# One-hot matmuls issued two list items behind their VectorE operations, with a third buffer for the gated one-hots

## The chip, the core and the metric

One core of a Trainium2 chip runs one program: a two-layer network over 512 tokens. The metric is device time in microseconds (us) of one execution. A core has TensorE (PE in the profile: matmuls; PEld: its weight loads), VectorE (DVE), ScalarE (ACT), GpSimd (POOL) and SyncE (SP). Each works through a queue of its own in program order; semaphores hold an instruction back until what it reads is written and what it overwrites has been read.

## The reference, cut to what matters

Both layers end in a product-key mixture of 16384 experts. For every token, 8 heads pick 16 experts each, with a softmax gate:

```python
best_s, best_pos = lax.top_k(cand_s, PEER_TOPK)
idx = jnp.take_along_axis(cand_i, best_pos, axis=-1)
gate = jax.nn.softmax(best_s, axis=-1)
a = jnp.einsum('nd,nhkd->nhk', hb, u[ib])
w = gb * jax.nn.gelu(a, approximate=False)
out = jnp.einsum('nhk,nhkd->nd', w, v[ib])
```

The rest (a state-space mixer, windowed attention, norms, a gated add) is not touched.

## The kernel before, in words

`peer(L)` runs once a layer. Its 512 tokens are treated in two ways. For the first 128 the chosen rows of u and v are gathered by indirect transfers (`gather_step`, L669: GpSimd issues one row set at L695, VectorE multiplies and sums it four gather steps later at L678 for u or L687 for v; five row buffers). For the other 384 the experts are computed densely: 128 **u steps** (the loop at L982) each multiply one block of 128 experts with the 384 tokens, then 128 **v steps** add the weighted rows of v. What joins the two halves is G, the gates as a dense array of experts by tokens, which is made during the u steps.

One u step issues, in this order: `lin` (L986), 24 matmuls (lines L202 to L204, since each product is made of three with weights split in a high and a low part); the weights' split for a step two ahead is issued by `next_w` (high part on ScalarE, L169; low part on GpSimd in four pieces, L172); a Gelu on ScalarE (L993) and its store to DRAM; `gather(URATE)`, 1.17 gather steps on average; and `step(BRATE)`, which hands out work from a list.

That **list** (`bg`, L912) is written out by hand at L931 to L934. `T` items are top-16 searches of one head for 128 tokens, `D` items decode indices and gates of 128 tokens (four items), and `G_` items make G for four tokens each, 96 of them a layer. Every item has a cost (T 6.0, the two long D items 5.0 each, G 1.5), and a step hands out items until 2.65 is spent: somewhat under two G items a step. The list ends in a run of G items alone: `D(2)`, then 42 of them (10 and 32).

A G item's first part, `onehot(b)` (L878), is two VectorE operations: at L884 a compare of an iota with the indices, which writes the one-hots of 4 tokens to `early` (three buffers); at L886 their product with the gates, which writes `og` (two buffers, the pool's default). Its second part, `gmm(b)` (L889), is eight small matmuls (L898) that read both and add up G of the four tokens in one PSUM bank, a ScalarE copy (L899), and after every fourth item a transfer to DRAM (L902).

The loop at L936 decides the order. It runs an item's first part, lowers a counter of every pending second part, and issues those in front of the queue whose counter is 0:

```python
for cost, f, *late in items:
    g = f()
    for q in prev:
        q[0] -= 1
    while prev and prev[0][0] <= 0:
        prev.pop(0)[1]()
    if g is not None:
        prev.append([late[0] if late else 1, g])
    yield cost
```

The default count is 1: `gmm` of an item is issued right behind the VectorE operations of the next item, of whatever kind that is. Where a step hands out two G items i and i+1, TensorE's queue thus holds lin, gmm(i-1), gmm(i), next lin, and gmm(i) reads an `og` that VectorE makes in this same step.

Of the kernel before, what the change touches and what calls it, by code (L numbers as in the profile page):

```python
# [20 lines left out]
P = 128  # L21
# [13 lines left out]
QT = 4  # L35
GSCALE = 32768.0
F16 = _mybir.dt.float16
# [25 lines left out]
class Net:  # L63
# [576 lines left out]
    def peer(self, L):  # L640
# [106 lines left out]
        with ExitStack() as ctx:  # L747
            mp = ctx.enter_context(tc.tile_pool(name="pm", bufs=2, reuse_waits="tile"))
# [45 lines left out]
            def topk(jobs):  # L794
                v = {}
                one, two = [], []
                for n, (tt, hd) in enumerate(jobs):
                    v[n] = mp.tile([P, 2, TOPK], F32, name=f"tv{n}")
                    for c in range(2):
                        src = early[hd][:, first.index(tt), c] if tt in first else late[:, later.index(tt), hd, c]  # L800
                        one.append((src, v[n][:, c, :], idx[:, c, tt, hd, :]))
                top16(one)
                for n, (tt, hd) in enumerate(jobs):
                    cand = mp.tile([P, TOPK, TOPK], F32, name=f"cand{n}", bufs=1)
                    vt.tensor_tensor(cand, v[n][:, 0, :, None].to_broadcast([P, TOPK, TOPK]),
                                     v[n][:, 1, None, :].to_broadcast([P, TOPK, TOPK]), op=OP.add)
                    two.append((cand.rearrange("p a b -> p (a b)"), best[:, tt, hd, :], pos[:, tt, hd, :]))
                top16(two)
# [7 lines left out]
            def decode_g(tt):  # L816
                gt = mp.tile([P, HEADS, TOPK], F32, name="gt", bufs=1)
                vt.tensor_tensor(gt, best[:, tt], best[:, tt, :, 0:1].to_broadcast([P, HEADS, TOPK]), op=OP.subtract)
                dec[tt] = gt, []
                return lambda: nc.scalar.activation(gt, gt, AF.Exp, scale=self.rv[:, tt:tt + 1])  # L820

            def decode_i(tt, c):
                pi = mp.tile([P, HEADS, TOPK], U32, name="pi", bufs=1)
                if c == 0:
                    vt.tensor_single_scalar(pi, pos[:, tt], 4, op=OP.logical_shift_right)
                else:
                    vt.tensor_single_scalar(pi, pos[:, tt], 15, op=OP.bitwise_and)
                pb = mp.tile([P, TOPK, HEADS], F16, name="pb", bufs=1)
                vt.tensor_copy(pb, pi.rearrange("p h k -> p k h"))
                ib = mp.tile([P, TOPK, HEADS], F16, name="ib")  # L830
                vt.tensor_copy(ib, idx[:, c, tt].rearrange("p h a -> p a h"))
                eq = mp.tile([P, TOPK, HK], F16, name="eq", bufs=1)
                vt.tensor_tensor(eq.rearrange("p a (n q) -> p a n q", q=QT),  # L833
                                 fl(pb).rearrange("p (n q) -> p n q", q=QT)[:, None].to_broadcast([P, TOPK, HK // QT, QT]),
                                 i16[:, :, None, :].to_broadcast([P, TOPK, HK // QT, QT]), op=OP.is_equal)
                e4 = eq.rearrange("p a (k h) -> p a k h", h=HEADS)
                vt.tensor_tensor(e4, e4, ib[:, :, None, :].to_broadcast([P, TOPK, TOPK, HEADS]), op=OP.mult)  # L837
                n = TOPK // 2
                while n > 1:
                    vt.tensor_tensor(eq[:, :n], eq[:, :n], eq[:, n:2 * n], op=OP.add)  # L840
                    n //= 2
                f = mp.tile([P, HK], F32, name=f"fi{c}", bufs=1)
                vt.tensor_tensor(f, eq[:, 0], eq[:, 1], op=OP.add)
                dec[tt][1].append(f)

            def decode_e(tt):
                gt, fi = dec.pop(tt)
                sm = mp.tile([P, 2, HEADS], F32, name="sm")
                vt.tensor_reduce(sm[:, 0], gt, axis=AX.X, op=OP.add)
                vt.reciprocal(sm[:, 1], sm[:, 0])  # L850
                gk = mp.tile([P, TOPK, HEADS], F32, name="gk", bufs=1)
                vt.tensor_tensor(gk, gt.rearrange("p h k -> p k h"), sm[:, 1, None, :].to_broadcast([P, TOPK, HEADS]),
                                 op=OP.mult)
                if tt == 0:
                    ef = wg[:, 0]
                    vt.tensor_scalar(ef, fi[0], float(P), float(L * NBLK * P), op0=OP.mult, op1=OP.add)
                    vt.tensor_tensor(ef, ef, fi[1], op=OP.add)
                    vt.tensor_copy(eg, ef)
                    vt.tensor_copy(gate, fl(gk))

                def turn():
                    if tt == 0:
                        self.gi = 0
                        return
                    pt = self.bank(7)
                    for j, src in enumerate(fi + [fl(gk)]):
                        nc.tensor.transpose(pt[:, j * P:(j + 1) * P], src, self.ident)
                    ts = slice(tt * P - NG, (tt + 1) * P - NG)
                    two = lambda j: pt[:, j * P:(j + 1) * P, None].to_broadcast([P, P, 2])
                    for j in range(2):  # L870
                        nc.scalar.activation(iT[:, ts, j], two(j), AF.Copy)
                    nc.scalar.activation(gT[:, ts, 0], two(2), AF.Copy, scale=GSCALE)
                    vt.scalar_tensor_tensor(gT[:, ts, 1], two(2), GSCALE, gT[:, ts, 0], op0=OP.mult, op1=OP.subtract)
                return turn
# [2 lines left out]

            def onehot(b):  # L878
                o = mp.tile([P, QT, 2, P], F16, name="early", bufs=3)
                og = mp.tile([P, QT, 2, P], F16, name="og")  # L880
                ts = slice(QT * b - NG, QT * b - NG + QT)
                pairs = lambda ap: ap.rearrange("p t c (a d) -> p t c a d", d=2)
                alike = lambda ap: ap[:, ts, :, None, :].to_broadcast([P, QT, 2, P // 2, 2])
                vt.tensor_tensor(pairs(o), iota.rearrange("p (a d) -> p a d", d=2)[:, None, None].to_broadcast(  # L884
                    [P, QT, 2, P // 2, 2]), alike(iT), op=OP.is_equal)
                vt.tensor_tensor(pairs(og), pairs(o)[:, :, 0:1].to_broadcast([P, QT, 2, P // 2, 2]), alike(gT), op=OP.mult)  # L886
                return o, og
# [24 lines left out]
            def bg():  # L912
                items = []

                def T(tt, *hds):
                    for hd in hds:
                        items.append((6.0, lambda hd=hd: topk([(tt, hd)])))

                def D(tt):
                    items.append((0.3, lambda: decode_g(tt), 2))  # L920
                    items.append((5.0, lambda: decode_i(tt, 0)))
                    items.append((5.0, lambda: decode_i(tt, 1)))
                    items.append((0.8, lambda: decode_e(tt), 2))

                def G_(tt, lo, hi):
                    def one(b):
                        o = onehot(b)
                        return lambda: gmm(b, o)
                    for b in range(32 * tt + lo, 32 * tt + hi):
                        items.append((1.5, lambda b=b: one(b)))  # L930
                D(0), T(1, 0, 1), D(3), T(1, 2, 3, 4), G_(3, 0, 12), T(1, 5, 6), G_(3, 12, 20), T(1, 7), D(1)  # L931
                G_(3, 20, 28), T(2, 0), G_(3, 28, 32), T(2, 1), G_(1, 0, 4), T(2, 2), G_(1, 4, 8), T(2, 3)
                G_(1, 8, 12), T(2, 4), G_(1, 12, 16), T(2, 5), G_(1, 16, 20), T(2, 6), G_(1, 20, 22), T(2, 7), D(2)
                G_(1, 22, 32), G_(2, 0, 32)  # L934
                prev = []
# [9 lines that stand above are left out]
                yield 3.0  # L945
                for _, g in prev:
                    g()
# [58 lines left out]
        with vctx:  # L1006
            mp = vctx.enter_context(tc.tile_pool(name="pv", bufs=3, reuse_waits="tile"))
# [549 lines left out]
```

## Time and profile before

| | us |
|---|---|
| median of three runs (lowest, highest) | 3457.02 (3456.63, 3461.01) |
| the profiled execution, its own time | 3453.39 |
| its span from first to last instruction | 3451.6 |
| TensorE, share of the span with a matmul in it | 95% |
| VectorE busy | 77% |
| GpSimd busy | 57% |
| ScalarE busy | 42% |

The u steps of layer 0 lie at about 643 to 1255 us of the span, those of layer 1 at about 2203 to 2791 us; v steps follow each. In the rows, an arrow `out<-in` names the tiles an operation writes and reads; a wait row reads "who waited, for whom: us in total, times, longest". The granted clock is the share of TensorE's full speed (2.4 GHz) that it was given; 0.5 is its other level, 1.2 GHz.

### The profile page before, as it was taken

What the parts mean: (1) busy time and instruction counts of PE and PEld (TensorE: products, weight loads), DVE (VectorE), ACT (ScalarE), POOL (GpSimd) and SP (SyncE); (2) the same over time, 40 slices, a digit from 0 to 9 for tenths busy, and PEclk for the clock granted to TensorE, in tenths of its full rate; (3) what the DMA queues carried; (4) which work ended last, traced back from release to release, by engine and by line L of the source; (5) the groups of instructions that cost most, each with busy time, mean ns of one, the idle gap of its engine ahead of it and who ended that gap; (6) DMA issues with size and microseconds to landing.
All of it is one profiled execution on the core that took longest, in us unless ns stands there. A gap on an engine that the chain in (4) does not pass through costs nothing.

```text
span 3451.6 us, 52253 instructions
## 1 busy us (share of the span) xinstructions
PE 3291.1 (95%) x18814; PEld 3022.6 (88%) x18814; DVE 2672.6 (77%) x4880; ACT 1455.2 (42%) x2198; POOL 1953.3 (57%) x2168
## 2 busy tenths in 40 slices
PE   8999999989999999999998999999999999999997
PEld 5777777989998989999996668989998989999996
DVE  7667667899998737878777865899988737877775
ACT  4433434444445533333334553444445533333334
POOL 5444545789888884322217226688888884322214
PEclk9999999999999999999999999999999999999998
DMA  3222212488888999999983112488888989999982
GB/s 119 85 77 70 74 62 75 151 280 309 309 312 303 330 310 358 358 336 346 337 286 107 45 59 89 138 278 308 316 309 297 334 304 356 353 346 339 339 304 85
DMA packets 357300, 827.50 MB, mean 240 GB/s; under 512 B 30000, under 2 KB 196528, under 8 KB 350896
## 3 DMA queue, kind: packets, MB, share of 16 engines
q1 hardware_dynamic: 235136, 448.59, 40.3%
q0 software_dynamic: 73728, 268.47, 21.1%
q10 hardware_dynamic: 48176, 107.10, 8.2%
q8 instruction: 147, 2.41, 0.3%
q14 instruction: 113, 0.93, 0.1%
HBM read 717.09 MB, written 106.95 MB: 239 GB/s over the span
## 4 chain that ended last, share of the span: by engine, by line
PE 58%; DVE 25%; POOL 7%; issue 5%; DMA 4%; ACT 1%; SPq 0%; POOLq 0%; DVEq 0%; ACTq 0%
PE bank L202 17%; PE bank L203 17%; PE bank L204 17%; POOL wlo L172 6%; DVE row L678 4%; DVE early L884 3%; DVE og L886 2%; DMA row<-u,eg 2%; POOL row L695 2%; DVE eq L840 1%; PE bank L898 1%; DMA wraw<-ut 1%; PE bank L971 1%; DVE eq L833 1%; DVE eq L837 1%
## 5 line engine op out<-in xcount | busy, mean ns | idle before, releaser
L172 POOL TENSOR_TENSOR wlo<-wraw,whi 128x256 fp32r<-128x256 f32 x1564 | 1256.1, 835 | 564.4 <-ACT whi L169 513.1
L169 ACT ACTIVATE whi<-wraw 128x1024 fp32r<-128x1024 f32 x647 | 685.5, 1061 | 740.5 <-issue 316.3
L695 POOL DMA_INDIRECT row<-v,eg x256 | 310.0, 1211 | 716.8 <-DVE yg L687 700.2
L204 PE MATMUL bank<-hhi,wlo 128*128 128x384 f32 x2048 | 699.8, 342 | 13.3 <-POOL wlo L172 13.2
L202 PE MATMUL bank<-hhi,whi 128*128 128x384 f32 x2048 | 708.6, 346 | 0.7 <-ACT whi L169 0.7
L203 PE MATMUL bank<-hlo,whi 128*128 128x384 f32 x2048 | 697.3, 340 | 0.0
L203 PE MATMUL bank<-vlo,whi 128*128 128x384 f32 x2032 | 684.1, 337 | 6.1 <-DVE vlo L744 6.0
L202 PE MATMUL bank<-vhi,whi 128*128 128x384 f32 x2032 | 684.8, 337 | 0.8 <-ACT vhi L742 0.8
L204 PE MATMUL bank<-vhi,wlo 128*128 128x384 f32 x2032 | 683.6, 336 | 0.0
L172 DVE TENSOR_TENSOR wlo<-wraw,whi 128x1024 fp32r<-128x1024 f32 x256 | 313.3, 1224 | 148.6 <-ACT whi L169 147.5
L204 PEld LDWEIGHTS bank<-hhi,wlo 128*128 128x128 f32 x2048 | 392.0, 191 | 20.0 <-POOL wlo L172 19.8
L202 PEld LDWEIGHTS bank<-hhi,whi 128*128 128x128 f32 x2048 | 393.3, 192 | 1.0 <-ACT whi L169 1.0
L203 PEld LDWEIGHTS bank<-hlo,whi 128*128 128x128 f32 x2048 | 392.8, 192 | 0.0
L203 PEld LDWEIGHTS bank<-vlo,whi 128*128 128x128 f32 x2032 | 382.6, 188 | 8.2 <-DVE vlo L744 8.2
L202 PEld LDWEIGHTS bank<-vhi,whi 128*128 128x128 f32 x2032 | 382.6, 188 | 2.0 <-ACT vhi L742 1.5
L204 PEld LDWEIGHTS bank<-vhi,wlo 128*128 128x128 f32 x2032 | 382.4, 188 | 0.3 <-POOL wlo L172 0.3
L678 DVE SCALAR_TENSOR_TENSOR row<-row,pair 128x1024 f32<-128x1024 f32 x256 | 305.6, 1212 | 88.1 <-DMA row<-u,eg 87.6
L687 DVE SCALAR_TENSOR_TENSOR yg<-row,wg,yg 128x1024 f32<-128x1024 f32 x254 | 328.0, 1291 | 35.9 <-DMA row<-v,eg 35.8
L202 PE MATMUL bank<-z,whi 128*128 128x512 f32 x728 | 322.0, 442 | 3.4 <-DVE sg L1137 3.4
L695 POOL DMA_INDIRECT row<-u,eg x256 | 278.5, 1088 | 50.4 <-issue 29.1
L993 ACT ACTIVATE ga<-bank 128x384 f32<-128x384 f32 x256 | 125.3, 490 | 418.0 <-PE bank L204 409.0
L203 PE MATMUL bank<-z,whi 128*128 128x512 f32 x728 | 291.1, 400 | 4.7 <-DVE z L262 4.7
(322 smaller groups left out, 4863.6 us busy)
## 6 DMA issues: line engine op xcount, KB each, us to landing
wraw<-ut SPq DMA_DIRECT2D x256, 512.0 KB
wraw<-v SPq DMA_DIRECT2D x256, 512.0 KB
wraw<-wlin SPq DMA_DIRECT2D x135, 512.0 KB
GA<-ga ACTq DMA_DIRECT2D x256, 192.0 KB
G<-gsz ACTq DMA_DIRECT2D x48, 1024.0 KB
gv<-G SPq DMA_DIRECT2D x96, 512.0 KB
gsz<-GA SPq DMA_DIRECT2D x256, 192.0 KB
PJ<-nf ACTq DMA_DIRECT2D x16, 256.0 KB
```

The costliest lines, as they stand in the source:

```text
L169: nc.scalar.activation(hi, r, AF.Copy)
L172: self.lo_eng.tensor_tensor(lo[:, q:q + n], r[:, q:q + n], hi.bitcast(F32)[:, q:q + n], op=OP.subtract)
L202: mm(out, whi, xhi, start=start, stop=False)
L203: mm(out, whi, xlo, start=False, stop=False)
L204: mm(out, wlo, xhi, start=False, stop=stop)
L678: vt.scalar_tensor_tensor(r, r, 1.0, self.pair, op0=OP.mult, op1=OP.mult, accum_out=wg[:, 0, j:j + 1])
L687: vt.scalar_tensor_tensor(yg, r, wg[:, 0, j:j + 1], yg, op0=OP.mult, op1=OP.add)
L695: nc.gpsimd.indirect_dma_start(out=got[i], out_offset=None, in_=t["u"] if i < NJ else t["v"].rearrange("a p d -> (a p) d"), in_offset=bass ...
L833: vt.tensor_tensor(eq.rearrange("p a (n q) -> p a n q", q=QT), fl(pb).rearrange("p (n q) -> p n q", q=QT)[:, None].to_broadcast([P, TOPK, ...
L884: vt.tensor_tensor(pairs(o), iota.rearrange("p (a d) -> p a d", d=2)[:, None, None].to_broadcast([P, QT, 2, P // 2, 2]), alike(iT), op=OP. ...
L886: vt.tensor_tensor(pairs(og), pairs(o)[:, :, 0:1].to_broadcast([P, QT, 2, P // 2, 2]), alike(gT), op=OP.mult)
L993: nc.scalar.activation(ga[:, NG:], ps[:, NG:], AF.Gelu)
```

## The change

The count of a G item becomes 2, so its matmuls are issued behind the VectorE operations of the second item after it, and `og` has three buffers in place of two.

```diff
             def onehot(b):
                 o = mp.tile([P, QT, 2, P], F16, name="early", bufs=3)
-                og = mp.tile([P, QT, 2, P], F16, name="og")
+                og = mp.tile([P, QT, 2, P], F16, name="og", bufs=3)
...
                     for b in range(32 * tt + lo, 32 * tt + hi):
-                        items.append((1.5, lambda b=b: one(b)))
+                        items.append((1.5, lambda b=b: one(b), 2))
```

In a step with two G items i and i+1, TensorE's queue then holds lin, gmm(i-2), gmm(i-1), next lin. No instruction is added or taken away. As `early` keeps three buffers, the compare of item i overwrites what gmm(i-3) reads, which is now issued right ahead of that compare instead of one item earlier.

## Rows read from the trace of the kernel before

**Rows 1.** Busy time by engine over the span, from the page.

```profile
PE 3291.1 (95%) x18814; PEld 3022.6 (88%) x18814; DVE 2672.6 (77%) x4880; ACT 1455.2 (42%) x2198; POOL 1953.3 (57%) x2168
```

**Rows 2.** Busy time by stretch, three of each layer, then v steps.

```profile
core 0: us, PE busy (x) PEld busy (x) DVE busy (x) ACT busy (x) POOL busy (x), PEclk, DMA share, GB/s
...
725.00:1056.00 331.00, 307.88 (x2003) 300.10 (x2002) 313.43 (x590) 159.50 (x198) 288.29 (x338) 0.97 0.87 305
1056.00:1069.00 13.00, 8.68 (x52) 8.08 (x50) 11.60 (x20) 4.74 (x8) 11.69 (x12) 0.74 0.86 296
1069.00:1190.00 121.00, 113.52 (x843) 109.33 (x841) 105.48 (x131) 71.53 (x86) 104.54 (x114) 0.99 0.91 322
...
2285.00:2615.00 330.00, 309.02 (x2008) 301.23 (x2006) 303.64 (x592) 159.71 (x199) 292.34 (x339) 0.97 0.87 308
2615.00:2629.00 14.00, 8.07 (x47) 7.74 (x48) 11.82 (x20) 4.46 (x8) 9.62 (x12) 0.76 0.80 295
2629.00:2749.00 120.00, 113.81 (x846) 109.80 (x844) 102.66 (x132) 71.76 (x87) 105.79 (x114) 0.99 0.90 320
...
2900.00:3300.00 400.00, 400.00 (x2310) 400.00 (x2309) 319.49 (x385) 146.42 (x195) 113.16 (x92) 1.00 1.00 346
```

**Rows 3.** Waits over the whole span.

```profile
PE bank L898 <- DVE og L886: 63.3, 35, 3.7
...
DVE og L886 <- PE bank L898: 39.9, 31, 3.4
```

**Rows 4.** Timeline around one wait of TensorE (start us, us, engine, line).

```profile
1002.54 2.08 POOL L172 TENSOR_TENSOR wlo<-wraw,whi 128x256 fp32r<-128x256 f32 x3
1002.85 2.33 DVE L884 TENSOR_TENSOR early<-iota,iT 128x1024 f16<-128x1024 f16 x1
...
1005.28 0.69 DVE L886 TENSOR_TENSOR og<-early,gT 128x1024 f16<-128x1024 f16 x1
...
1006.03 1.03 PE L898 MATMUL bank<-og,early 128*128 128x128 f16 x8 [3.11 <-DVE og L886]
```

**Rows 5.** Waits in the first six stretches of Rows 2, in that order.

```profile
DVE og L886 <- PE bank L898: 6.7, 4, 3.4
...
DVE row L678 <- DMA row<-u,eg: 2.4, 2, 2.0
...
PE bank L898 <- DVE og L886: 3.8, 2, 2.7
...
DVE og L886 <- PE bank L898: 12.5, 11, 1.8
...
PE bank L898 <- DVE og L886: 7.5, 5, 2.1
...
DVE row L678 <- DMA row<-u,eg: 11.5, 7, 4.5
...
DVE og L886 <- PE bank L898: 6.8, 5, 2.0
...
PE bank L898 <- DVE og L886: 4.8, 2, 3.7
...
DVE og L886 <- PE bank L898: 13.8, 11, 2.0
...
PE bank L898 <- DVE og L886: 6.2, 4, 2.1
```

**Rows 6.** Groups of 725 to 1195 us; last, line L886 over the span.

```profile
L884 DVE TENSOR_TENSOR early<-iota,iT 128x1024 f16<-128x1024 f16 x96 | 118.8, 1238 | 0.0
L886 DVE TENSOR_TENSOR og<-early,gT 128x1024 f16<-128x1024 f16 x96 | 94.6, 985 | 27.9 <-PE bank L898 19.3 <-issue 0.5
...
L172 POOL TENSOR_TENSOR wlo<-wraw,whi 128x256 fp32r<-128x256 f32 x362 | 290.5, 835 | 42.2 <-ACT whi L169 40.2 <-issue 0.8
...
L886 DVE TENSOR_TENSOR og<-early,gT x192: 691/694/3519, 729.8 to 2744.2; 128x1024 f16<-128x1024 f16 x192
```

## The prediction

> **What bounds the kernel now.** I read the busy times of the whole span first, then the waits, then the busy times by stretch, then one wait in the timeline. Over the span TensorE is at 95% and VectorE at 77% [rows 1]. That mean hides two regimes: in the v steps TensorE is busy without a gap (400 of 400 us) and VectorE has a fifth of its time free; in the u steps with list items VectorE is busy 313.4 of 331 us in layer 0 and 303.6 of 330 us in layer 1, more than TensorE is [rows 2]. So the change acts only in the u steps, and what it is worth there is asked of VectorE as well as of TensorE.
>
> The two wait for each other at the same pair of lines: TensorE waits 63.3 us in 35 places for the gated one-hots (L898 on L886), and VectorE 39.9 us in 31 places until the small matmuls have read an old buffer (L886 on L898) [rows 3]. One case shows how it goes: a weight split on GpSimd starts at 1002.54, the compare beside it takes 2.33 us, the product ends at 1005.97, and the matmuls start at 1006.03 after a wait of 3.11 us [rows 4]. Such stops also cost clock: granted were 0.97 of full speed in the mixed stretches and 0.74 in the step of the last decode, which holds such a wait, against 1.00 in the v steps, so part of those stretches ran at 1.2 of 2.4 GHz [rows 2]. So one late operation of VectorE stops TensorE at once, as the matmuls of an item stand in the very step that makes it; then TensorE is late and VectorE waits for it.
>
> I cut the list into three stretches per layer [rows 2]: the mixed list (331 and 330 us), the step of the last decode (13 and 14 us), and G items alone (121 and 120 us).
>
> **The change, part by part.** No instruction is added, so no busy time is. What moves is `gmm`: eight small matmuls, one ScalarE copy and, on every fourth item, one store from ScalarE's queue go one item later. SP's and GpSimd's queues hold nothing of it. The later ScalarE copy costs nothing: it stands in its queue behind a matmul that is now ready, where before ScalarE waited with TensorE. At the list's end two groups instead of one are left over; they go out in that step or the next, at about 1190 us in layer 0, where the u steps go on to 1255 before G is read.
>
> What TensorE's waits become: in a step with two G items the last group now needs the previous step's one-hots. VectorE may be most of a step late before TensorE stops.
>
> What VectorE's waits become: the compare of item i now overwrites what gmm(i-3) reads, which is issued just ahead of it, so the limit that keeps VectorE from running ahead comes one operation earlier, at L884 and no longer at L886. Queued behind a waiting compare are the product and the next gather's multiply, and TensorE needs that product only two items later. I cost this at nothing where VectorE is late anyway. Cover gone, each of the 31 waits grows by one compare, 1.24 us by its mean [rows 6]: 38 us of VectorE's time, the bound from above.
>
> **The sum, by stretch.** *Mixed list.* VectorE is the bound: of 331 us it is idle 17.6, of which 6.7 wait for TensorE and 2.4 for gathered rows; layer 1: 26.4 idle, 6.8 and 11.5 [rows 2, 5]. TensorE's own waits here (63.3 less the other stretches' 22.3, so 41.0 us [rows 3, 5]) are no gain: VectorE has the work to do whether TensorE waits or not. What can go is VectorE's wait for TensorE, which follows on TensorE's stops: 6.7 + 6.8 = **13.5 us**. The waits for rows (13.9 us) may shrink, since a stopped TensorE makes ScalarE late and GpSimd behind it, which issues the gathers; bounds 0 and 13.9, and I take 0, as most gathers wait on nothing here.
>
> *Last decode and G items alone.* TensorE loses 3.8 us in waits and 13 x (1 - 0.74) = 3.4 us of clock, then 7.5 and 121 x 0.01 = 1.2: 15.9 us; layer 1: 4.8, 3.4, 6.2 and 1.2, so 15.6 [rows 2, 5]. Together 31.5 us, if TensorE is let go. VectorE's own waits for it here are 12.5 + 13.8 = 26.3 us [rows 5]; with 105.5 of 121 us busy it enters this stretch late by up to a step and has little to catch up with. The smaller of the two counts: **26.3 us**.
>
> Together 13.5 + 26.3 = **39.8 us, taken as 40**. The v steps take it over whole: they are bound by TensorE and start earlier. The profiled execution took 3453.4 us (span 3451.6), 3.6 below the median of 3457.0; from the first the sum gives 3413.4, against the median **3417**.
>
> **A rule weighed.** The compare and the product take 118.8 + 94.6 us in layer 0, against 192 x 0.691 = 132.7 undisturbed: 81 us go to meetings with GpSimd's splits, and the longest single product took 3.519 us, where one piece of a split takes 0.835 [rows 6]. I price a bad meeting by that row, at 3.52 - 0.69 = 2.8 us. The Trainium skill, page "SBUF — State Buffer", section "Who interferes with whom", says that a VectorE instruction with two SBUF inputs and a GpSimd instruction that reads SBUF exclude each other, and that whoever issues first holds the port for that whole instruction. By that a bad meeting would cost one piece, 0.84 us, and the slower case below would need 48 more of them in place of 14; the row of 3.519 us differs, and the measurement decides.
>
> **The rivals.**
> *VectorE bounds all of it.* If VectorE is late all through and what it saves in the mixed list comes back as waits for rows or at L884, only TensorE's stops in the run of G items alone go: 7.5 + 6.2 + 2.4 of clock = 16 us, 3441. For it: VectorE's 95% in layer 0's mixed list. Against: the 26 us in which it waits with nothing else in its way.
>
> *TensorE bounds all of it.* Then every wait goes, 63.3 us, and with it the clock it costs, 2 x (9.9 + 3.4 + 1.2) = 29 us: 92 us, 3365. Against: VectorE would need 331 - 22.2 - 9.9 us or less in a stretch where it is busy 313.4. A half-way case is likelier: 40, the 13.9 us of rows and 31.5 - 26.3 = 5.2 of lag, 59 us, 3398. The page "TensorE: Matmul & The Clock Gate", section "HAM oscillation", of the Trainium skill puts the loss of a throttled stretch at half its time, on top of the wait; by it alone one would take the 92.
>
> *Slower: more meetings of one-hots and splits.* GpSimd now waits 40.2 us for ScalarE in layer 0's window [rows 6], partly behind TensorE's stops. Without them its splits come closer together, and VectorE starts the compare behind a matmul group, at a fixed place against the splits. Place: L884 and L886 against L172. Price: an operation that is caught by a whole burst of four pieces costs the 2.8 us above. The gain is gone when 14 more of the 384 are caught (40 / 2.8); if the 81 us a layer grow by half, 81 us in both, the time is 3457 - 40 + 81 = 3498. Against: the splits' share of the time (290.5 of 470 us) rises by no more than the stretch shrinks, 4%, worth some 3 us a layer.
>
> *It doesn't do what it says.* The wait moves along: matmuls wait one step later for the same operation, as VectorE's lateness is lasting, and VectorE waits at L884 as long as it did at L886 and one compare more, the 38 us that bound its cost above. Then 40 - 38 = 2 us are left: 3455, no change.
>
> **How the numbers follow.** A measurement here tells some 0.2%, 7 us, from no change. Chances: the forecast (25 to 50 us) 0.48; VectorE bounds all (8 to 25) 0.20; the half-way and the TensorE case (over 50) 0.13; no change 0.10; slower 0.09. Faster: 0.48 + 0.20 + 0.13 = 0.81. The range leaves out slower, half of no change and the part of the fast cases over 67 us: from 3390 (40 + 13.9 + 13, of which 5.2 is lag and the rest collisions that fail to happen) to 3450 (a gain of 7).
>
> **What would show it.** Right: waits of L898 on L886 fall from 63.3 us to under 25; VectorE's waits on L898 appear at L884 and total under 10; the step of the last decode is shorter by some 6 us a layer, the run of G items alone takes about 114 us in place of 121 and 120, with VectorE 92% busy in it (105.5 of 114); v steps unchanged. Wrong: L884 waits of 40 us or more; a mean of L884 or L886 well over 1.24 and 0.99 us; or VectorE's waits for rows growing by what the others lose.

## The result and the profile after

The changed kernel takes 3431.07 us (median of four runs, 3430.10 to 3436.78), the one before on the same chip 3456.82 us: a ratio of 0.9925, 95% interval 0.9909 to 0.9941. That is 26 us less (20 to 31), where 40 was forecast.

The page of the changed kernel, its span and the busy times that answer to [rows 1]:

```profile
span 3428.5 us, 52077 instructions
...
PE 3281.8 (96%) x18814; PEld 3007.1 (88%) x18814; DVE 2712.8 (79%) x4880; ACT 1452.7 (42%) x2198; POOL 1968.1 (57%) x2168
```

TensorE is busy 9 us less; its mean granted clock rose from 0.983 to 0.988, which fits. VectorE is busy 40 us more (2672.6 before), with the same 4880 instructions. That second number is the story of this change.

The u steps, cut where the list ends (the last product of one-hots and gates), first for the kernel before: list and rest of layer 0, then of layer 1. The columns are as in [rows 2].

```profile
core 0: us, PE busy (x) PEld busy (x) DVE busy (x) ACT busy (x) POOL busy (x), PEclk, DMA share, GB/s
637.00:1187.00 550.00, 512.65 (x3362) 499.73 (x3361) 511.30 (x991) 275.44 (x346) 476.09 (x544) 0.97 0.85 295
1187.00:1280.00 93.00, 89.15 (x504) 85.31 (x502) 33.88 (x46) 32.87 (x45) 82.28 (x101) 1.00 0.91 314
2198.00:2745.00 547.00, 511.40 (x3355) 498.91 (x3355) 497.32 (x987) 274.86 (x346) 476.48 (x544) 0.97 0.85 296
2745.00:2840.00 95.00, 89.42 (x507) 85.92 (x505) 34.79 (x47) 33.11 (x45) 84.76 (x101) 1.00 0.90 311
```

The same four stretches of the changed kernel:

```profile
634.00:1172.00 538.00, 509.92 (x3370) 494.88 (x3369) 523.74 (x989) 273.44 (x345) 484.34 (x544) 0.98 0.87 301
1172.00:1263.00 91.00, 86.42 (x495) 82.85 (x493) 34.40 (x47) 33.40 (x46) 82.20 (x100) 1.00 0.91 318
2186.00:2724.00 538.00, 509.09 (x3371) 492.58 (x3370) 523.34 (x991) 273.62 (x345) 488.61 (x544) 0.99 0.86 302
2724.00:2817.00 93.00, 86.42 (x494) 82.85 (x493) 35.67 (x47) 33.70 (x46) 84.37 (x101) 1.00 0.89 311
```

The lists take 1076 us in place of 1097, and the steps behind them 184 in place of 188. So the gain lies in the u steps, most of it in the list. There VectorE's busy time rose from 1008.6 to 1047.0 us, and its idle time fell from 88.4 to 28.9 us: 97% busy, it bounds the list from end to end. The share of full clock went from 0.97 to 0.98 and 0.99.

Six stretches of the changed kernel that end at the same u steps as those of [rows 2] (there the first of layer 0 and of layer 1 was cut some 5 to 6 us ahead of a step's end, at 725 and 2285 for steps that ended at 730.4 and 2291.0), and 400 us of v steps:

```profile
726.00:1044.00 318.00, 300.68 (x1973) 291.16 (x1973) 309.52 (x581) 158.86 (x198) 288.60 (x330) 0.98 0.89 312
1044.00:1056.00 12.00, 8.05 (x41) 7.61 (x41) 11.86 (x15) 3.35 (x7) 11.18 (x16) 0.72 0.89 303
1056.00:1172.50 116.50, 112.47 (x844) 108.07 (x842) 115.05 (x135) 70.94 (x86) 106.28 (x109) 1.00 0.93 333
2278.00:2593.60 315.60, 299.20 (x1973) 288.29 (x1974) 306.65 (x588) 157.84 (x197) 294.49 (x332) 0.99 0.90 315
2593.60:2603.00 9.40, 6.54 (x36) 6.15 (x35) 9.30 (x10) 3.35 (x6) 8.76 (x10) 0.82 0.81 289
2603.00:2724.00 121.00, 113.96 (x846) 109.43 (x846) 119.59 (x133) 70.72 (x85) 108.66 (x114) 0.99 0.91 328
2880.00:3280.00 400.00, 400.00 (x2309) 400.00 (x2309) 320.68 (x385) 144.93 (x195) 107.34 (x92) 1.00 1.00 345
```

The mixed list takes 318.0 and 315.6 us. The run of G items alone takes 116.5 and 121.0 us, where VectorE was busy 105.5 and 102.7 us before and is now 115.1 and 119.6. The v steps are as they were.

Waits of the changed kernel over the whole span (who waited, for whom: us, times, longest), to be held against [rows 3]:

```profile
DVE row L678 <- DMA row<-u,eg: 72.3, 29, 6.2
...
PE bank L898 <- DVE og L886: 42.0, 30, 3.5
...
DVE early L884 <- PE bank L898: 0.9, 1, 0.9
```

VectorE's 39.9 us of waiting for TensorE are gone but for 0.9. TensorE's 63.3 us fell to 42.0.

The one-hot operations, first before, then after, over both layers (busy us, mean ns, then idle time ahead of them):

```profile
L884 DVE TENSOR_TENSOR early<-iota,iT 128x1024 f16<-128x1024 f16 x192 | 227.5, 1185 | 0.0
L886 DVE TENSOR_TENSOR og<-early,gT 128x1024 f16<-128x1024 f16 x192 | 186.4, 971 | 56.7 <-PE bank L898 39.9 <-issue 0.5
```

```profile
L884 DVE TENSOR_TENSOR early<-iota,iT 128x1024 f16<-128x1024 f16 x192 | 242.6, 1263 | 0.9 <-PE bank L898 0.9
L886 DVE TENSOR_TENSOR og<-early,gT 128x1024 f16<-128x1024 f16 x192 | 214.1, 1115 | 6.6
```

Compare and product together went from 413.9 to 456.7 us: 43 us more for the same 384 operations. The idle time ahead of the product holds a small gain besides: 56.7 us before, of which 39.9 and 0.5 have a name; 6.6 us now. The separate semaphore instruction that stood ahead of 188 of the 192 products is no longer in the trace; that the product has one thing less to wait for is the likely reason.

Which operations got longer can be counted in the two traces. A one-hot that overlaps no weight split takes 0.689 us on average, before (153 of the 384) and after (113): all of the extra time lies in those that overlap one, 231 before and 271 after. Sorted by length, 141 one-hots took 0.8 to 1.5 us before and 189 after, and 38 and 43 took longer. The middle group brings some 26 of the 43 us, the long ones some 18.

How the lag works where it works is seen in the timeline of the changed kernel (start us, us, engine, line):

```profile
1096.42 2.80 POOL L172 TENSOR_TENSOR wlo<-wraw,whi 128x256 fp32r<-128x256 f32 x4
...
1097.36 2.42 DVE L884 TENSOR_TENSOR early<-iota,iT 128x1024 f16<-128x1024 f16 x1
...
1099.82 0.69 DVE L886 TENSOR_TENSOR og<-early,gT 128x1024 f16<-128x1024 f16 x1
...
1100.63 4.07 POOL L172 TENSOR_TENSOR wlo<-wraw,whi 128x256 fp32r<-128x256 f32 x4
...
1101.14 1.11 DVE L886 TENSOR_TENSOR og<-early,gT 128x1024 f16<-128x1024 f16 x1
...
1101.72 1.22 PE L898 MATMUL bank<-og,early 128*128 128x128 f16 x16
```

A split of four pieces runs from 1096.42, and the compare beside it takes 2.42 us, as the one in [rows 4] did. The next two groups of matmuls start at 1101.72 without a wait, though the product of 1101.14 isn't finished: they read older one-hots. That product shows the milder kind of meeting. It starts inside the second burst of four pieces and ends after 1.11 us, with the burst still running; the burst takes 4.07 us where the first took 2.80.

### The profile page after: what moved, and what is told of

Read it like the earlier page. It is cut to its first block, busy times and chain, and to the rows that moved or that the text cites. A ratio compares the mean times of both kernels' runs of the same rounds, so it can differ in the third digit from the quotient of the medians.

```text
span 3428.5 us, 52077 instructions
## 1 busy us (share of the span) xinstructions
PE 3281.8 (96%) x18814; PEld 3007.1 (88%) x18814; DVE 2712.8 (79%) x4880; ACT 1452.7 (42%) x2198; POOL 1968.1 (57%) x2168
## 4 chain that ended last, share of the span: by engine, by line
PE 54%; DVE 32%; POOL 5%; DMA 4%; issue 3%; ACT 1%; POOLq 0%; SPq 0%; ACTq 0%; DVEq 0%
PE bank L202 16%; PE bank L203 16%; PE bank L204 16%; DVE row L678 6%; DVE early L884 6%; DVE og L886 5%; POOL wlo L172 4%; DMA row<-u,eg 2%; DVE eq L840 1%; POOL row L695 1%; DMA wraw<-v 1%; PE bank L971 1%; DVE eq L837 1%; DVE eq L833 1%; DMA wraw<-ut 1%
## 5 line engine op out<-in xcount | busy, mean ns | idle before, releaser
L172 POOL TENSOR_TENSOR wlo<-wraw,whi 128x256 fp32r<-128x256 f32 x1564 | 1279.4, 850 | 517.3 <-ACT whi L169 468.3
L172 DVE TENSOR_TENSOR wlo<-wraw,whi 128x1024 fp32r<-128x1024 f32 x256 | 313.4, 1224 | 159.4 <-ACT whi L169 158.3
L678 DVE SCALAR_TENSOR_TENSOR row<-row,pair 128x1024 f32<-128x1024 f32 x256 | 305.2, 1212 | 72.6 <-DMA row<-u,eg 72.3
L204 PE MATMUL bank<-z,wlo 128*128 128x512 f32 x728 | 290.1, 399 | 0.0
```

Source lines behind the costliest of these rows:

```text
L172: self.lo_eng.tensor_tensor(lo[:, q:q + n], r[:, q:q + n], hi.bitcast(F32)[:, q:q + n], op=OP.subtract)
L204: mm(out, wlo, xhi, start=False, stop=stop)
L678: vt.scalar_tensor_tensor(r, r, 1.0, self.pair, op0=OP.mult, op1=OP.mult, accum_out=wg[:, 0, j:j + 1])
```

## The experiments

**1. The third buffer alone.**

```diff
-                og = mp.tile([P, QT, 2, P], F16, name="og")
+                og = mp.tile([P, QT, 2, P], F16, name="og", bufs=3)
```

> The third buffer of the gated one-hots alone, matmuls still one item behind. Theory A (what the second item of lag saved in VectorE's waits came back in part as longer one-hot operations, because more of them meet GpSimd's weight splits): the buffer alone lets the product start early but TensorE still waits for it in the same step, so 3440 to 3457 us, TensorE's waits of L898 on L886 at 50 us or more. Rival B (the one-hots got longer through the third buffer itself, its place in SBUF): L884 and L886 together rise from 414 us towards 457 us here too, and the time is 3457 or above. Rival C (the buffer is what brings the gain, not the lag): 3431 us.

Measured: 3447.56 us, ratio 0.9969 (0.9952 to 0.9986), some 11 us less than before (5 to 17). The profiled execution is the fastest of ten, 3436.30 us. Its list stretches, one-hot lines and waits:

```profile
635.00:1174.00 539.00, 506.52 (x3346) 493.19 (x3345) 512.83 (x988) 272.92 (x342) 478.24 (x540) 0.98 0.85 298
...
2190.00:2727.00 537.00, 505.22 (x3345) 492.21 (x3344) 508.04 (x990) 272.38 (x342) 472.22 (x539) 0.98 0.85 299
...
L884 DVE TENSOR_TENSOR early<-iota,iT 128x1024 f16<-128x1024 f16 x192 | 235.1, 1224 | 0.6 <-PE bank L898 0.5
L886 DVE TENSOR_TENSOR og<-early,gT 128x1024 f16<-128x1024 f16 x192 | 192.1, 1001 | 6.6
...
DVE row L678 <- DMA row<-u,eg: 110.2, 56, 8.7
...
PE bank L898 <- DVE og L886: 57.8, 34, 3.4
...
DVE early L884 <- PE bank L898: 0.5, 2, 0.3
```

VectorE's waits for TensorE are gone here already (0.5 us). TensorE still waits 57.8 us, and VectorE's waits for gathered rows rose from 87.6 to 110.2 us over the span. So the buffer alone ends VectorE's waits for TensorE, and by its ratio it is worth about 11 of the 26 us. What the lag adds is not placed by this profile: in this fast execution the lists took 1076 us, as in the changed kernel (1097 before), and the steps behind them 194 us (184 in the changed kernel, 188 before). Theory A's time and wait hold. One-hots rose by 13 us only (427.2), and those that overlap no split took 0.689 us here too, so rival B (the buffer's place) falls. Rival C (the buffer alone brings it) falls by the times, whose intervals lie apart. The lag alone, with two buffers, wasn't tried: the product of item i would overwrite what a group behind it in TensorE's queue has still to read.

**2 and 3. Few splits, one and two items behind.** In both, `next_w` makes one piece of four for the weights of 124 of the 128 u steps, and `lin` takes the high part where the low part is missing, so this kernel computes another result:

```diff
-            for q in range(0, D, n):
+            for q in range(0, n if short else D, n):
...
-            self.mm3(ps, whi[:, s], wlo[:, s], h[k][0], h[k][1], k == 0, k == len(h) - 1)
+            self.mm3(ps, whi[:, s], (whi if len(w) > 2 and k > 1 else wlo)[:, s], h[k][0], h[k][1], k == 0,
+                     k == len(h) - 1)
```

> One item behind as before, but in the u steps GpSimd makes only the first quarter of each low part (one piece of four; the matmuls take the high part in place of the rest, so the count of matmuls stays and the result is another). Theory A (meetings with splits are what makes one-hots late): L884 and L886 together fall from 414 to under 320 us, TensorE's waits for L886 from 63 to under 25 us, time 3380 to 3410 us. Rival B (one-hots are long for a reason of their own): they stay over 390 us, waits over 50 us, time over 3440.

> The same with matmuls two items behind and the third buffer. Theory A: L884 and L886 together fall from 457 to under 320 us, VectorE is no longer the bound, TensorE's waits for L886 under 10 us, time 3370 to 3400 us, 3 to 20 us under the run one item behind: without long meetings the second item of lag has little left to do. Rival B: one-hots stay over 430 us and the time within 10 us of 3431.

Measured: 3323.83 us one behind (0.9616, 0.9591 to 0.9641) and 3322.79 us two behind (0.9613, 0.9587 to 0.9638). One behind (these lines stand four further down: L888 is the compare, L890 the product, L902 the matmuls):

```profile
L890 DVE TENSOR_TENSOR og<-early,gT 128x1024 f16<-128x1024 f16 x192 | 139.3, 725 | 131.2 <-PE bank L902 117.9 <-DVE early L888 0.5
L888 DVE TENSOR_TENSOR early<-iota,iT 128x1024 f16<-128x1024 f16 x192 | 138.0, 719 | 0.0
...
PE bank L902 <- DVE og L890: 1.7, 2, 0.8
```

Two behind, with layer 0's list in the last row:

```profile
L890 DVE TENSOR_TENSOR og<-early,gT 128x1024 f16<-128x1024 f16 x192 | 139.6, 727 | 6.6
L888 DVE TENSOR_TENSOR early<-iota,iT 128x1024 f16<-128x1024 f16 x192 | 134.5, 700 | 121.6 <-PE bank L902 120.8
...
637.00:1130.00 493.00, 493.00 (x3335) 483.06 (x3334) 400.92 (x981) 269.74 (x339) 212.35 (x229) 1.00 0.92 327
```

With a quarter of the pieces the one-hots take 277.3 and 274.1 us, near the 265 of 384 undisturbed ones at 0.691. TensorE's waits for them are 1.7 us one behind, and none are listed two behind; two behind, TensorE is busy for all of the 493 us at a granted clock of 1.00, and it is VectorE that waits (120.8 us over both layers). So the meetings with GpSimd's splits were what made one-hots late, and not the order in which they are issued: rival B falls. Without them the second item of lag is worth 1 us, which these intervals can't tell from nothing. The time fell much further than either expectation said (3370 at best). The other VectorE operations, and GpSimd itself, were relieved as well; how the 108 us under the changed kernel divide among these wasn't taken apart.

**4. The list spread over more steps.**

```diff
-URATE, VRATE, BRATE = 1.17, 0.94, 2.65
+URATE, VRATE, BRATE = 1.17, 0.94, 2.45
```

> The changed kernel with 2.45 in place of 2.65 spent on list items per u step, so that the list lasts some nine steps longer and each step holds less VectorE work; nothing else changes. Theory A (VectorE bounds the u steps with list items, TensorE those behind the list): TensorE's waits for L886 fall from 42 to under 25 us and the time by 8 to 25 us, to 3406 to 3423. Rival D (TensorE's speed bounds it already, VectorE only looks full): the time stays within 0.2% of 3431.

Measured: 3412.38 us, 0.9867 (0.9831 to 0.9902). Its waits:

```profile
PE bank L898 <- DVE og L886: 25.0, 14, 3.1
...
DVE early L884 <- PE bank L898: 3.3, 3, 1.6
```

Less VectorE work in each step, and TensorE waits less: VectorE was the bound (theory A). The wait of 25.0 us came out at the limit named and not under it.

**5 and 6. Splits in smaller and larger pieces.** `LOP = 4` becomes 8 and 2 on the changed kernel.

> The changed kernel with each GpSimd split of a low part in eight pieces of 128 columns in place of four of 256. Theory A1 (an operation that meets a split waits for the piece that runs, at most): with pieces half as long the extra of a met one-hot halves, L884 and L886 together fall from 457 to under 400 us and the time to 3395 to 3420 us, unless GpSimd's own time per piece grows. Theory A2 (an operation can be kept out by a whole burst of pieces): the one-hots stay at 440 us or more, and as GpSimd pays eight starts in place of four the time is 3431 to 3460.

> The changed kernel with each split in two pieces of 512. Theory A1 (wait for the piece that runs): the extra of a met one-hot doubles, L884 and L886 together rise from 457 to over 520 us and the time to 3445 to 3480. Theory A2 (kept out by the whole burst): one-hots within 30 us of 457 and the time within 10 us of 3431.

Measured: 3529.44 us with eight pieces (1.0212, 1.0191 to 1.0234), 3455.29 us with two (0.9991, 0.9981 to 1.0000). Eight pieces of 128 (the row with three times per operation gives the least, the median and the longest):

```profile
L884 DVE TENSOR_TENSOR early<-iota,iT 128x1024 f16<-128x1024 f16 x192 | 289.7, 1509 | 7.8 <-PE bank L898 7.8
L886 DVE TENSOR_TENSOR og<-early,gT 128x1024 f16<-128x1024 f16 x192 | 173.0, 901 | 6.6
...
L172 POOL TENSOR_TENSOR wlo<-wraw,whi 128x128 fp32r<-128x128 f32 x3128 | 1523.6, 522 | 387.9 <-ACT whi L169 353.2 <-PE bank L971 30.0
...
L884 DVE TENSOR_TENSOR early<-iota,iT x192: 675/750/4142, 724.2 to 2797.4; 128x1024 f16<-128x1024 f16 x192
...
PE bank L204 <- POOL wlo L172: 61.2, 82, 2.8
```

The one-hots stay at 462.7 us, and the longest compare takes 4.142 us beside pieces of 0.522 on average: an operation can be kept out by a whole burst (theory A2). Not every one is: 151 of them took 0.8 to 1.5 us, and 69 longer. The time went past A2's 3460. GpSimd's splits grew by 19% (1523.6 us, 1279.4 in the changed kernel), and TensorE waits 61.2 us for low parts (19.3 in the changed kernel); how the loss divides between the two wasn't taken apart. Two pieces of 512:

```profile
L884 DVE TENSOR_TENSOR early<-iota,iT 128x1024 f16<-128x1024 f16 x192 | 222.3, 1158 | 1.7 <-PE bank L898 1.7
L886 DVE TENSOR_TENSOR og<-early,gT 128x1024 f16<-128x1024 f16 x192 | 200.0, 1042 | 6.6
...
L852 DVE TENSOR_TENSOR gk<-gt,sm 128x128 f32<-128x128 f32 x8 | 14.9, 1859 | 0.3
...
PE 3283.6 (95%) x18814; PEld 3018.9 (87%) x18814; DVE 2781.5 (81%) x4880; ACT 1452.2 (42%) x2198; POOL 1769.8 (51%) x1386
```

Neither theory holds here. The one-hots got shorter, 422.3 us against 456.7, where A1 wanted over 520; but VectorE as a whole is busy 2781.5 us against 2712.8, as other operations take longer: the eight gate products of L852 take 1859 ns on average, 499 in the changed kernel. Six of the eight overlap a split here and take 2353 ns, the other two 377. Pieces of 256 are the best of the three.

**7 to 9. VectorE relieved in other ways, on the changed kernel.** The three rates (gather steps per u and per v step, list cost per u step) become 1.06, 1.0, 2.65, then 1.06, 1.0, 2.45, then 1.06, 1.0, 2.40.

> The changed kernel with 1.06 gather steps per u step in place of 1.17, and 1.0 per v step in place of 0.94, so that each u step holds 0.11 fewer multiplies of gathered rows (1.21 us each on VectorE) and the v steps take them. Theory A (VectorE bounds the u steps with list items): 113 steps x 0.11 x 1.3 us = 16 us less VectorE work a layer ahead of the list's end, the time falls by 15 to 32 us, to 3399 to 3416. Rival D (TensorE or the transfers bound them): within 0.2% of 3431.

> Both: 2.45 of list items and 1.06 gather steps per u step, 1.0 per v step, on the changed kernel. Theory A: the two reliefs of VectorE add up until TensorE is the bound: 3385 to 3405 us, TensorE's waits for L886 under 15 us. If TensorE bounds from the first relief on (2.45 alone gave 3412), no more than 5 us come on top: 3407 to 3412.

> Two items behind with 2.40 in place of 2.45 of list items per u step (1.06 and 1.0 kept): the list lasts two steps longer. If VectorE still bounds the list: 2 to 8 us below 3396.5. If TensorE is the bound or the end of the list comes too near to the first use of G: 3395 to 3410.

Measured: 3405.56 us (0.9844, 0.9828 to 0.9861), 3396.53 us (0.9822, 0.9804 to 0.9839) and 3386.61 us (0.9777, 0.9756 to 0.9799). Waits of the last:

```profile
DVE early L884 <- PE bank L898: 18.7, 12, 3.3
...
PE bank L898 <- DVE og L886: 15.8, 7, 3.1
```

Each relief of VectorE shortened the program (a gather that moves to the v steps takes an issue off GpSimd in the u steps as well). The first two times are as theory A had them, though in the second TensorE's waits stayed at 28.3 us, above the 15 named; the third step brought 10 us by the medians where 2 to 8 were expected. With 2.40 both kernels are beaten, the one before by 2.2%; both engines now wait 16 to 19 us for each other.

**10 and 11. What lag and buffer are worth at the relieved rates** (1.06, 1.0, 2.45): both taken back, and the lag alone taken back.

> The rates of the last run (2.45, 1.06, 1.0) on the kernel before: one item behind, two buffers. Theory A (at the old rates the list is bound by VectorE, which hides most of what the lag gives TensorE): with VectorE relieved the lag and the buffer are worth more than the 26 us they brought, 30 to 45, so 3427 to 3441 us here against 3396.5. Rival E (a relieved VectorE is late less often, so there is less for a lag to cover): 3400 to 3418 us.

> The same rates, three buffers, one item behind. Theory A: the third buffer gives VectorE its waits back, the lag lets TensorE go; with VectorE relieved the lag is the larger part, so 3408 to 3425 us, 12 to 28 above 3396.5. Rival E: 3397 to 3405 us.

Measured: 3421.38 us (0.9883, 0.9858 to 0.9908) with neither, 3413.77 us (0.9864, 0.9829 to 0.9899) with the buffer alone, against 3396.53 with both. With neither:

```profile
DVE og L886 <- PE bank L898: 49.0, 29, 6.3
...
PE bank L898 <- DVE og L886: 40.4, 22, 3.9
```

The pair is worth 25 us here by the medians, about what it was at the old rates. The run with both was taken on another chip; by the ratios to the kernel before, measured beside each, it is 21 us, give or take 10. So neither the 30 us at which theory A begins nor rival E (3.5 to 21.5 us by its times) is excluded. By the medians the buffer makes 8 of them and the lag 17, as in the first experiment, but the intervals with neither and with the buffer alone overlap for the most part, so the 8 us are not told from nothing. That VectorE at the old rates hides most of what the lag gives is not borne out. One-hots grow again, from 429.5 us with neither to 456.6 with the buffer alone and 465.3 with both: here most of the growth comes with the buffer, where at the old rates it brought 13 of 43 us.

## Why the prediction was right in its sign and too high in its gain

**The place.** Right: the gain lies in the u steps, the v steps run as before (400 of 400 us busy), and VectorE bounds the list.

**VectorE's waits for TensorE.** Forecast to go, 39.8 us; 39.0 went. They moved to L884 as said, and there are 0.9 us of them, not the 38 that bounded them from above.

**The step that failed: "No instruction is added, so no busy time is."** VectorE's busy time in the lists grew by 38.4 us: the one-hots alone by 43, and other operations gave a little back. The prediction had this mechanism as its slower rival, at L884 and L886 against L172, and sized it by the splits' share of the time at "some 3 us a layer". It measured about 21 a layer. That the splits are what lengthens them is shown by the runs with few splits, where the same lag leaves the one-hots at 274 us, and by the 0.689 us of those that overlap none. Why the meetings cost more once VectorE doesn't stop stays open. An engine that is never idle has no more pauses in which a split can pass without meeting anything, which would fit the rise from 231 to 271 meetings. At the relieved rates, though, the meetings fell from 285 with neither change to 269 with both, while those over 1.5 us rose from 37 to 52. No run separates this from a mere shift of the two engines against each other.

**Gains that were taken as nothing.** Waits for rows: from 3.4 + 13.4 to 2.7 + 4.1 us in the lists, 10 us, within the bounds of 0 and 13.9. The idle time ahead of the product that no releaser explains: 16.3 to 6.6 us, 10 us, not foreseen. The lead that TensorE has at the list's end: 4 us, against 5.2 in the half-way rival. So 39 + 10 + 10 + 4 - 38 = 25; 25.75 was measured, and the profiled executions differ by 23. That the time fell inside the range is in part luck: two gains of 10 us, taken as nothing or not foreseen, made up for half of a loss that had been put at nothing. The gain of 26 us lies at the lower edge of the forecast's 25 to 50, next to the rival in which VectorE bounds all of it (8 to 25).

**The two counts of the last stretch.** Cut at the ends of the same steps, the mixed list went from 325.9 to 318.0 us (730.4 to 1056.3, now 725.7 to 1043.7) and from 323.7 to 315.7 (2291.0 to 2614.7, now 2277.9 to 2593.6): 15.9 us, against 13.5 forecast. The step of the last decode gave 0.5 us (12.5 to 12.0) and 4.6 (14.1 to 9.5), the run of G items 3.7 (120.5 to 116.8) and -2.2 (119.0 to 121.2): together 6.6 us where 26.3 were forecast, and here the shortfall lies. To take the smaller of TensorE's 31.5 and VectorE's 26.3 us was sound, but both were counted with the durations of before: VectorE's waits were filled by 26.5 us more work (105.5 + 102.7 to 115.1 + 119.6). Seven more one-hots fall into the two runs of G items (157 in place of 150), and each takes 1.13 us on average where it took 1.00.

**What was to show it.** The waits at L884 came out as said. TensorE's waits of 42.0 us are above the 25 named: with VectorE as the bound, TensorE has to wait somewhere. The last decode gave 0.5 and 4.6 us where some 6 a layer were named, and the run of G items took 116.8 and 121.2 us where 114 was, with VectorE 99% busy in it and not 92%. The mean of the product, 1115 ns against 985 in [rows 6] (971 over both layers), is the sign that was named for "wrong".

**The rule that was weighed.** Both prices occur. The prediction took 2.8 us a meeting, by which 14 more would have eaten the gain; the long meetings rose by 5 only, from 38 to 43, and what grew most was the meetings of 0.8 to 1.5 us, about one piece, from 141 to 189. But one piece is not the limit either: with pieces of 0.522 us on average an operation still took 4.142 us. The page "SBUF — State Buffer" of the Trainium skill, section "Who interferes with whom", is borne out in that one-hots and splits exclude each other, and not, for the long ones, in the wait for a single instruction.

One reading ahead of the prediction was off: the u steps run to 1280 us in layer 0 and to 2840 in layer 1, not to 1255 and 2791, by the last Gelu at L993. No term of the sum used it.

## What to carry to other kernels

Where two engines hold each other up by turns, test a buffer more and an item of lag apart; here the buffer alone ended VectorE's waits for TensorE, and the lag then brought TensorE's own waits from 57.8 to 42.0 us. Ask too whether the engine that no longer pauses will lose more time to what keeps it out: here it did, at both sets of rates. Before the gain of a removed wait is booked, ask how much of the bounding engine's busy time is itself waiting: here an operation of 0.69 us took 1.2 on average. Where lateness comes from such meetings, fewer of them or less work per step may bring more than a deeper order of issue: here a quarter of the splits brought 133 us (with another result), and the three rates at their best some 45 us under the changed kernel.

## What the runs showed of the hardware

One-hots that overlap no split took 0.69 us on average in every run here. Beside a burst of four GpSimd pieces, in the kernel before and the changed one, there were two outcomes. Most of those that were held up took 0.8 to 1.5 us, the time of about one piece more. The long ones (38 and 43) ended only when the burst was over, after up to 3.57 and 3.74 us beside pieces of some 0.73 us; beside a burst of eight pieces of some 0.45 us it was up to 4.14 us. By the profile the longest began 0.1 to 0.4 us ahead of the burst's first piece, so starting first did not give them their turn. What decides between the two outcomes no run here shows. GpSimd pays as well: the piece of 256 columns took 712 ns at the least and 850 on average, and halving the piece raised the whole from 1279 to 1524 us.

The multiply of gathered rows at L678, which reads one of its inputs from PSUM, was not held up: in the changed kernel it took 1.211 us in the 216 cases that overlap a split and 1.214 in the other 40.
